# Regrouping the column widths of a streaming skewness kernel: 31 loads instead of 27, same bytes

## Chip, cores and metric

The kernel runs on one core of a Trainium2 chip. The metric is the device time of one execution in microseconds. Unless said otherwise, a quoted time is the median of a kernel's runs. "Faster" or "slower" ask for more than 2%, which is 1.8 us here.

## The reference

```python
rows, cols = 1024, 8192                      # x: float32, standard normal
mean = np.mean(x, axis=-1, keepdims=True)
std = np.std(x, axis=-1, keepdims=True)
z = (x - mean) / (std + 1e-8)
return np.mean(z ** 3, axis=-1)              # skewness of each row
```

## The kernel before

The 1024 rows are eight blocks of 128 rows. Each block of 8192 columns is loaded in tiles of the widths in `UNITS`. For each tile, ACT squares it and sums the squares, DVE multiplies the squares by x and sums the cubes, and PE transposes it into an accumulator for the sum of x. Tiles wider than 2304 columns are squared and cubed in two pieces.

```python
UNITS = [
    [4096, 4096], [4096, 4096], [4096, 4096], [4096, 4096],
    [3584, 2304, 2304],
    [2304, 2304, 2048, 1536],
    [1664, 1792, 1920, 1664, 1152],
    [1024, 1024, 1152, 1280, 1408, 1152, 1152],
]
SUB_MAX = 2304
X_BUFS = 8
# ... cut ...
xt = xpool.tile([P, w], FP, tag="x", name=f"x_{b}_{k}")
nc.sync.dma_start(out=xt, in_=xv[b, :, c0 : c0 + w])            # L140
for s, e in _slices(w):
    # sq is in SBUF; in PSUM ("sqps") for the very last tile
    nc.scalar.activation(out=sq, in_=xt[:, s:e], func=AF.Square,  # L147
        scale=s_scale, accum_out=s2u[:, j : j + 1])
    nc.vector.scalar_tensor_tensor(out=cube, in0=sq, scalar=1.0,  # L152
        in1=xt[:, s:e], op0=ALU.mult, op1=ALU.mult,
        accum_out=s3u[:, j : j + 1])
# ... PE transposes of xt into tp (L165) ...
# after each block: tsb <- tp (ACT, L174), s1ps <- tsb x ones (PE, L175)
# blocks 6 and 7 are closed by small ACT steps (L123 to L128), the last one writes s3u;
# then num <- sum of s3u (DVE, L189), skew (DVE, L192), output DMA (L193)
```

Of the kernel before, what the change touches and what calls it, by code (L numbers as in the profile page):

```python
# [14 lines left out]
UNITS = [  # L15
    [4096, 4096],
    [4096, 4096],
    [4096, 4096],
    [4096, 4096],
    [3584, 2304, 2304],  # L20
    [2304, 2304, 2048, 1536],
    [1664, 1792, 1920, 1664, 1152],
    [1024, 1024, 1152, 1280, 1408, 1152, 1152],
]
S1_ACT = {(0, 0): 1024, (1, 0): 1024, (2, 0): 1024}
SUB_MAX = 2304
# [197 lines left out]
```

## Time and profile before

| | before |
|---|---|
| median time | 91.67 us (91.57 to 91.84, 3 runs); with the later runs of the comparison 91.71 us |
| span in the profile | 89.7 us |
| DMA: rate at 8:40 us, rate at 67:77 us | 429, 413 GB/s |
| last tile landed | 83.56 us |
| DVE's last cube done, ACT's last correction done | 86.60, 86.73 us |
| output DMA issued | 87.23 us |

The prediction below reads the profile's lines of this kernel. Two habits matter. A busy share says little where four engines are all near 80%: what counts is which wait ends last. And a full DMA row tells that nothing is gained by feeding the queue better. The landing times in this document are the trace's own record of the completion of each load.

### The profile page before, as it was taken

How to read it: one execution, taken by the hardware profiler on the slowest of the kernel's cores; microseconds unless marked ns; L12 is line 12 of the kernel's file. 1: busy time of each engine (PE TensorE's matmuls, PEld its weight loads, DVE VectorE, ACT ScalarE, POOL GpSimd, SP SyncE). 2: the span in 40 equal slices, each digit the busy share in tenths (PEclk: the TensorE clock that was granted, in tenths of full speed). 3: DMA queues.
4: the chain of work that ended last, by engine and by line, in shares of the span. 5: the costliest groups of instructions: out<-in, count | busy, mean ns of one | idle time of the engine just before them, and what ended most of it. 6: DMA issues, size and time to landing. Idle time of an engine off the chain costs nothing.

```text
span 89.7 us, 1368 instructions
## 1 busy us (share of the span) xinstructions
PE 64.9 (72%) x504; PEld 59.3 (66%) x504; DVE 72.7 (81%) x80; ACT 72.1 (80%) x106; POOL 11.3 (13%) x14
## 2 busy tenths in 40 slices
PE   0003999892882919989998988888987798969710
PEld 0003999791872909979897977877876787848500
DVE  1000498989999298995999999999999999999970
ACT  6003999699991999859898989978979898999950
POOL 3000000000000000000000000000005999900030
PEclk9999999999999997599999999999999999999998
DMA  3999999999999999999999999999999999994000
GB/s 117 351 424 438 424 431 431 431 431 424 446 416 431 424 438 424 424 438 427 415 409 418 419 427 419 421 415 419 409 414 417 404 413 411 421 412 161 0 0 2
DMA packets 4038, 33.64 MB, mean 375 GB/s; under 512 B 576, under 2 KB 576, under 8 KB 2240
## 3 DMA queue, kind: packets, MB, share of 16 engines
q1 hardware_dynamic: 4032, 33.56, 89.7%
q8 instruction: 4, 0.07, 0.3%
q14 instruction: 2, 0.02, 0.0%
HBM read 33.55 MB, written 0.00 MB: 374 GB/s over the span
## 4 chain that ended last, share of the span: by engine, by line
DMA 73%; ACT 13%; issue 5%; DVE 4%; SPq 1%; PE 1%; DVEq 0%; ACTq 0%
DMA x<-in_x_dram 73%; ACT sq L147 9%; DVE sq L152 3%; ACT sqps L147 1%; ACT same L159 1%; SPq L140 1%; PE s1ps L175 1%; ACT tsb L174 0%; ACT s3u L128 0%; ACT v L127 0%; ACT var L125 0%; DVE num L189 0%; ACT m1sq L124 0%; DVE skew L192 0%; ACT nm L126 0%
## 5 line engine op out<-in xcount | busy, mean ns | idle before, releaser
L152 DVE SCALAR_TENSOR_TENSOR sq<-sq,x 128x2048 f32<-128x2048 f32 (+9 forms) x35 | 70.7, 2071 | 13.4 <-ACT sq L147 13.3
L165 PE MATMUL tp<-ident,x 128*128 128x128 f32 x488 | 62.6, 288 | 17.3 <-DMA x<-in_x_dram 17.2
L165 PEld LDWEIGHTS tp<-ident,x 128*128 128x128 f32 x488 | 57.9, 150 | 20.9 <-DMA x<-in_x_dram 12.7
L147 ACT ACTIVATE sq<-x 128x2048 f32<-128x2048 f32 (+9 forms) x35 | 60.6, 1734 | 10.7 <-DMA x<-in_x_dram 9.9
L110 POOL TENSOR_TENSOR vara<-m2a,m1sqa 128x6 f32<-128x6 f32 x1 | 1.8, 1822 | 67.1 <-DVE m3a L99 67.1
L147 ACT ACTIVATION_READ_ACCUMULATOR sq<-x 128x1 f32 x35 | 6.5, 186 | 0.0
L175 PEld LDWEIGHTS s1ps<-onesn,tsb 128*128 128x128 f32 x16 | 2.4, 188 | 5.2 <-ACT tsb L174 5.2
L175 PE MATMUL s1ps<-onesn,tsb 128*128 128x1 f32 x16 | 3.1, 260 | 3.3 <-ACT tsb L174 3.3
L174 ACT COPY tsb<-tp 128x128 f32<-128x128 f32 x8 | 2.0, 256 | 2.0 <-PE tp L165 2.0
L114 POOL TENSOR_TENSOR rra<-vara,expo 128x6 f32<-128x6 f32 x1 | 3.3, 3267 | 0.0
L159 ACT ACTIVATE same<-x 128x1024 f32<-128x1024 f32 x3 | 3.1, 1041 | 0.0
L152 DVE DVE_READ_ACCUMULATOR sq<-sq,x 128x1 f32 x35 | 2.9, 83 | 0.0
L111 POOL TENSOR_TENSOR m1sq3a<-m1sq3a,vara 128x6 f32<-128x6 f32 x1 | 1.9, 1868 | 0.1
L77 ACT ACT_TABLE_LOAD x1 | 1.3, 1283 | 0.7 <-PEq L208 0.7
L187 POOL TENSOR_TENSOR rr<-var,expo 128x2 f32<-128x2 f32 x1 | 0.7, 702 | 7.7 <-ACT var L125 7.7
L152 DVE SCALAR_TENSOR_TENSOR cube<-sqps,x 128x1152 f32<-128x1152 f32 x1 | 1.4, 1350 | 0.0
L113 POOL TENSOR_TENSOR m3a<-m3a,m1sq3a 128x6 f32<-128x6 f32 x1 | 1.2, 1201 | 0.1
L147 ACT ACTIVATE sqps<-x 128x1152 f32<-128x1152 f32 x1 | 1.1, 1136 | 0.1
L115 POOL TENSOR_TENSOR skew<-m3a,rra 128x6 f32<-128x6 f32 x1 | 1.1, 1069 | 0.1
L124 ACT ACTIVATE m1sq<-s1ps 128x1 f32<-128x1 f32 x2 | 0.3, 171 | 0.5 <-PE s1ps L175 0.5
L75 DVE MEMSET onesn<- 128x1 f32 x1 | 0.1, 59 | 0.8 <-PEq L208 0.8
L112 POOL TENSOR_TENSOR m1sq3a<-m1sq3a,nm1a 128x6 f32<-128x6 f32 x1 | 0.7, 697 | 0.0
(28 smaller groups left out, 6.8 us busy)
## 6 DMA issues: line engine op xcount, KB each, us to landing
x<-in_x_dram SPq DMA_DIRECT2D x8, 2048.0 KB, 23.4
x<-in_x_dram SPq DMA_DIRECT2D x4, 1152.0 KB, 27.9
x<-in_x_dram SPq DMA_DIRECT2D x4, 576.0 KB, 8.6
x<-in_x_dram SPq DMA_DIRECT2D x1, 1792.0 KB, 33.0
x<-in_x_dram SPq DMA_DIRECT2D x2, 832.0 KB, 13.9
x<-in_x_dram SPq DMA_DIRECT2D x1, 1024.0 KB, 21.1
x<-in_x_dram SPq DMA_DIRECT2D x2, 512.0 KB, 10.0
x<-in_x_dram SPq DMA_DIRECT2D x1, 960.0 KB, 13.2
```

The lines of the kernel that those rows point to most:

```text
L77: nc.scalar.activation(out=tiny, in_=onesn, func=AF.Square)
L110: g.tensor_tensor(out=var, in0=m2, in1=m1sq, op=ALU.subtract)
L111: g.tensor_tensor(out=m1sq3, in0=m1sq3, in1=var, op=ALU.add)
L113: g.tensor_tensor(out=m3, in0=m3, in1=m1sq3, op=ALU.add)
L114: g.tensor_tensor(out=rr, in0=var, in1=expo, op=ALU.pow)
L115: g.tensor_tensor(out=skew[:, 0:F], in0=m3, in1=rr, op=ALU.mult)
L147: nc.scalar.activation(out=sq, in_=xt[:, s:e], func=AF.Square, scale=s_scale, accum_out=s2u[:, j : j + 1],)
L152: nc.vector.scalar_tensor_tensor(out=cube, in0=sq, scalar=1.0, in1=xt[:, s:e], op0=ALU.mult, op1=ALU.mult, accum_out=s3u[:, j : j + 1],)
L159: nc.scalar.activation(out=same[:, 0:w_act], in_=xt[:, w - w_act : w], func=AF.Copy, scale=inv_n, accum_out=s1a[:, b : b + 1],)
L165: nc.tensor.matmul(out=tp, lhsT=xt[:, c * P : (c + 1) * P], rhs=ident, start=(k == 0 and c == 0), stop=(c0 == C and c == n - 1), is_transp ...
L174: nc.scalar.copy(out=tsb, in_=tp)
L175: nc.tensor.matmul(out=s1ps[:, b : b + 1], lhsT=tsb, rhs=onesn, start=True, stop=True)
```

## The change

Its apparent intent is to let tiles shrink earlier, so that ACT and DVE wait less for whole 2 MB tiles, and to end on a narrower tile. Nothing but the list of widths changes.

```diff
 UNITS = [
     [4096, 4096],
     [4096, 4096],
-    [4096, 4096],
-    [4096, 4096],
-    [3584, 2304, 2304],
-    [2304, 2304, 2048, 1536],
-    [1664, 1792, 1920, 1664, 1152],
-    [1024, 1024, 1152, 1280, 1408, 1152, 1152],
+    [3456, 1792, 2944],
+    [2944, 2304, 2944],
+    [2944, 2688, 2560],
+    [1920, 1920, 1792, 1536, 1024],
+    [1536, 1408, 1408, 1152, 1408, 1280],
+    [1152, 1152, 1408, 1152, 1280, 1152, 896],
 ]
```

## The prediction

> **What bounds the kernel now.** I began with the page's activity in 40 slices, because four engines are busy 72 to 81% of the span and none of them is the limit by share alone.
>
> ```profile
> DVE  1000498989999298995999999999999999999970
> ACT  6003999699991999859898989978979898999950
> DMA  3999999999999999999999999999999999994000
> GB/s 117 351 424 438 424 431 431 431 431 424 446 416 431 424 438 424 424 438 427 415 409 418 419 427 419 421 415 419 409 414 417 404 413 411 421 412 161 0 0 2
> ```
>
> One digit is a slice of 2.24 us. The DMA row is full from slice 1 to slice 35: there is no hole that another order of transfers could fill. DVE and ACT have holes, and they lie early (slices 10, 12, 18), where they wait for whole 2 MB tiles. The second thing to see is that the rate sinks from about 430 to about 412 GB/s while the transfers become narrower.
>
> The chain that ended last, on the page and then in order of time:
>
> ```profile
> DMA 73%; ACT 13%; issue 5%; DVE 4%; SPq 1%; PE 1%; DVEq 0%; ACTq 0%
> ...
> 76.01 0.02 SPq L140
> 76.03 0.03 issue
> 76.06 7.50 DMA x<-in_x_dram
> 83.56 0.02 issue
> 83.58 1.26 ACT sqps L147 x2
> 84.84 0.00 issue
> 84.84 0.28 ACT tsb L174
> ...
> 86.44 0.30 ACT s3u L128
> 86.74 0.02 issue
> 86.76 0.18 DVE num L189
> ```
>
> So: loading ends at 83.56 us, then follows a serial tail, of which only the first 1.26 us (the squares of the last 1152 columns) depends on the widths. The stretch from 84.84 to the end is fixed small work. The chain goes through a DVE-released buffer at 76.06, but that issue lands 7.5 us later: behind it stood five more transfers of block 7 (1152+1280+1408+1152+1152 = 6144 columns, 3.15 MB, 7.6 us at 412 GB/s). The queue was full, so the buffer wait cost nothing.
>
> Last, the end of DVE in the timeline of the last microseconds:
>
> ```profile
> 83.58 1.14 ACT L147 ACTIVATE sqps<-x 128x1152 f32<-128x1152 f32 x1
> ...
> 85.24 1.35 DVE L152 SCALAR_TENSOR_TENSOR cube<-sqps,x 128x1152 f32<-128x1152 f32 x1
> ...
> 86.52 0.08 DVE L152 DVE_READ_ACCUMULATOR cube<-sqps,x 128x1 f32 x1
> 86.76 0.17 DVE L189 TENSOR_REDUCE num<-s3u 128x2 f32<-128x16 f32 x1 [0.16 <-ACT s3u L128]
> ```
>
> DVE is done at 86.60, ACT's last correction at 86.74: DVE is 0.14 us from being the limit, since it starts the last cube at 85.24, half a microsecond after ACT has the squares (84.75). The list of waits puts 13.3 us of DVE idle on ACT, 9.2 of it before the first tile; the other 4.1 us lie before 41.4 us.
>
> **What the Trainium skill says.** "DMA: Bandwidth & Descriptors", section "Where 436 GB/s comes from", gives 435 GB/s as the ceiling of the SBUF ports; the trace's 429 to 434 GB/s in the wide stretch stands right below it. The same page, section "Why small descriptors are slow (HBM only)", says that each packet carries a fixed overhead; the trace agrees in kind and gives the size used below. "Perfetto Trace Analysis", section "DMA Optimizations", says that splitting may help if the DMA engines are generally idle; here they are not. "ScalarE: Activation LUTs", section "What ACT_TABLE_LOAD costs", gives 186 ns + 0.833 ns per column for an ACTIVATE, back-to-back ones overlapping by 93 ns: 1146 ns for 1152 columns, where the trace has 1136 to 1155.
>
> **The change, part by part.** Bytes, matmuls and the small work stay.
>
> (1) Transfers: 27 become 31. Each has 128 rows, and the packet count (4032 on the queue = 27x128 rows + 128 output rows + 28x16 completions) shows one packet per row, eight per DMA engine. I price a packet from two windows of the DMA view. From 8 to 40 us: 838 row packets of 16 KB (934 less 96 small ones), 16 engines x 32 us x 1.003 = 513.5 engine-us, 613 ns each. From 67 to 77 us: 817 row packets, 4.13 MB, so 5055 B each, 16 x 10 x 1.017 = 162.7 engine-us, 199 ns each. A straight line through both has 0.0365 ns per byte and 15 ns per packet. Check: 58 to 67 us has 532 packets of 7030 B in 144.4 engine-us, 271 ns each; the line says 271. Hence a transfer costs 8 x 15 = 0.12 us plus 1.17 ns per column. Four more transfers: 4 x 0.12 = **+0.47 us** on the landing of the last one. This is fully on the path, because DMA never rests.
>
> (2) Slices: pieces over 2304 columns are halved. Before: 4x4+4+4+5+7 = 36. After: 4+4+5+5+6+5+6+7 = 42, six more. In the timeline an ACT slice costs 0.833 ns per column + 0.20 us from start to start (1.27 for 1280), a DVE slice 1.04 + 0.08 us (1.42 for 1280). So ACT gets 6 x 0.20 = 1.2 us and DVE 6 x 0.08 = 0.5 us. Both lie beside DMA: a block of 8192 columns takes DMA about 9.8 us, ACT 6.8 + 5 x 0.2 + some 0.5 = 8.3 (+1.05 in the first three blocks for the partial sum), DVE 8.5 + 5 x 0.08 = 8.9. They stay below it. **0 on the path.**
>
> (3) The last width: 1152 becomes 896. The squares shrink by 256 x 0.833 = **-0.21 us**, if ACT is free when it lands. With the transfer cost of (1), the last four widths 1152, 1280, 1152, 896 land at L-4.23, L-2.62, L-1.16 and L. ACT takes 1.27 for the 1280 (to L-1.33) and 1.16 for the 1152 from its landing (to L+0.0). ACT is free just in time, so the saving counts. DVE, even if it runs without a gap, ends the 1280 at about L+0.4, the 1152 at L+1.7 and the 896 at L+2.7; ACT's correction comes at 3.18-0.21 = L+2.97. So ACT still closes.
>
> (4) Earlier landings in blocks 2 to 4: a first tile of 3456 instead of 4096 lands 640 x 1.17 = 0.75 us earlier, and the first of block 3 some 1152 x 1.17 = 1.3 us. That fills part of DVE's early idle, and about pays for the 0.5 us of new slice cost. Its backlog does not carry the end, so **0** again.
>
> Sum: +0.47 - 0.21 = +0.26 us on 91.67, or 91.93. I choose a little less, **91.85**, because the falling rate may in part be a drift: 433, 429, 428 GB/s in the windows 8:18, 18:28, 28:38, where the width does not change.
>
> **The rivals.** (a) *The granularity gain is real*: early idle of ACT and DVE (4.1 us of DVE) vanishes and the time falls with it. For it: the holes in their rows, and the page on splitting. Against: their idle is not on the chain; DMA is full while they wait. At best DVE's 0.14 us distance grows. If in addition packets cost nothing extra, the time is 91.67-0.21 = 91.45. (b) *Buffer starvation*: eight buffers hold fewer bytes when the tiles are narrow, and the queue runs dry. For it: 64.2 us of waits for DVE in the queue's own list. Against: block 7 of before already ran so, with five transfers of about 1200 columns ahead, 7 us of work, while DMA stayed full. The changed blocks 4 to 6 are wider than that, 1024 to 2944. A dry spell would cost 1 to 3 us: 93 to 95. (c) *DVE becomes the bound*: it runs without a hole from 43 us to 86, and gets 29 slices instead of 24 in blocks 3 to 7, +0.4 us. If it gained nothing from (4), its end would be 86.60 + 0.4 - 0.27 (shorter last cube) = 86.73, still no later than L+2.97 = 87.0. Only a lag in ACT, as when the granted clock dipped to 0.83 from 28 to 38 us and the copy of the sums waited 1.48 us for PE, could make this worse; I give it +0.3.
>
> **Range and chances.** Between rival (a) with free packets (91.45, less 0.2 for run to run) and my sum with rival (c) (92.2, plus 0.2) lies the range 91.2 to 92.5. Two per cent is 1.83 us. Faster than 89.84 would need the landing at 81.7 at an unchanged tail, with loads that fill the ports already: 1 to 2%. Slower than 93.5 needs (b): 2 to 3%.
>
> **What would show it.** In the changed profile: the DMA row full to the end of loading; 4608 packets on the queue (31x128 + 128 + 32x16) and a last landing near 84.0 (step 1); rates of 416 to 424 where blocks 2 to 4 travel, instead of about 428; 41 + 1 squares and cubes (step 2); an ACT sqps of about 0.92 us that starts within 0.1 us of the landing (step 3); fewer DVE holes in slices 12 to 18 (step 4); the closing reduction still released by ACT. The prediction is wrong if the DMA row shows a gap, if the last landing comes earlier than 83.4, or if the reduction is released by DVE's cube.

## The result, and the profile after

The changed kernel took 91.89 us (median of 4 runs, 91.88 to 92.15), the kernel before 91.71 us in the same comparison. The ratio is 1.0027, with a 95% interval of 1.0004 to 1.0050. A ratio is the mean time of one kernel's runs over that of the other's of the same rounds, so it is not quite the ratio of the medians. The change costs about 0.25 us. The predicted 91.85 us was right to 0.04 us, and the outcome lies within 2%.

From the page of the changed kernel, activity of DVE and DMA in 40 slices of 2.25 us:

```profile
DVE  1000598989899597999998999999999999779980
DMA  4899999999999999999999999999999999994000
```

DMA is full to the end of loading, as before. DVE's early holes are shallower, but it has new ones in slices 34 and 35 (77 to 81 us), just where nothing can be made up any more. Its total wait for ACT is 13.3 us in both kernels: idle time was moved, not removed.

The chain that ended last, from the page and in order of time:

```profile
DMA 52%; issue 13%; DVE 12%; ACT 10%; PE 9%; SPq 1%; DVEq 0%; ACTq 0%
...
84.91 1.36 DVE sq L152 x3
86.28 1.02 DVE cube L152 x2
```

The chain no longer ends on a landing followed by ACT: it ends on DVE's cubes. The timeline of the last block (start, duration, instruction, and in brackets the idle time of the engine before it and who ended it) shows how that came about:

```profile
77.32 1.36 DVE L152 SCALAR_TENSOR_TENSOR sq<-sq,x 128x1152 f32<-128x1152 f32 x1 [0.38 <-ACT sq L147]
77.83 0.29 ACT L128 ACTIVATE s3u<-v,nm 128x1 f32<-128x1 f32 x1
78.03 1.15 ACT L147 ACTIVATE sq<-x 128x1152 f32<-128x1152 f32 x1
79.31 1.36 DVE L152 SCALAR_TENSOR_TENSOR sq<-sq,x 128x1152 f32<-128x1152 f32 x1 [0.62 <-ACT sq L147]
84.10 0.90 ACT L147 ACTIVATE sqps<-x 128x896 f32<-128x896 f32 x1
86.19 1.09 DVE L152 SCALAR_TENSOR_TENSOR cube<-sqps,x 128x896 f32<-128x896 f32 x1
86.60 0.29 ACT L128 ACTIVATE s3u<-v,nm 128x1 f32<-128x1 f32 x1
87.39 0.17 DVE L189 TENSOR_REDUCE num<-s3u 128x2 f32<-128x16 f32 x1
```

DVE waits 0.38 and 0.62 us for the squares of the first two tiles of block 7; from 79.31 on it works without a gap to 87.28. ACT's last correction is done at 86.89. Before, the last two stood at 86.60 and 86.73, with ACT closing. For comparison, the second tile of block 7 in before:

```profile
77.22 1.04 ACT L147 ACTIVATE sq<-x 128x1024 f32<-128x1024 f32 x1
78.26 0.28 ACT L128 ACTIVATE s3u<-v,nm 128x1 f32<-128x1 f32 x1
78.39 1.22 DVE L152 SCALAR_TENSOR_TENSOR sq<-sq,x 128x1024 f32<-128x1024 f32 x1
```

The squares of this tile start 0.81 us later in the changed kernel (78.03 against 77.22) and the cube 0.92 us later (79.31 against 78.39). The order of ACT's instructions differs too: before, the last small step of block 6 (L128) comes after these squares, in the changed kernel ahead of them. Of the 0.81 us, 0.38 were there when the first tile's squares started, 0.12 are their greater width, and 0.31 lie between the two tiles, where that step now stands.

One more difference lies behind the computation. In the list of waits of the sync engine, the wait for the output's DMA at the end of the program is 1.1 us in before and 0.8 us after, though the output takes 1.4 us from issue to landing in both. First before, then after:

```profile
SPq L219 <- DMA out_dram<-skew: 1.1, 1, 1.1
```

```profile
SPq L219 <- DMA out_dram<-skew: 0.8, 1, 0.8
```

So three things moved, and between the two profiled runs they add up:

| | before | after | difference |
|---|---|---|---|
| last tile landed | 83.56 | 83.85 | +0.29 |
| from there to the closing reduction | 3.20 | 3.54 | +0.34 |
| from the output's landing to the end | 1.08 | 0.83 | -0.25 |
| time of these two runs | 91.50 | 91.88 | +0.38 |

The profiled run of before, 91.50 us, was faster than the four runs of the comparison (91.57 to 91.84), hence +0.38 here and +0.25 over all runs. A landing scatters from one execution to the next: the five other kernels with 27 large loads in the trials below landed their last tile between 83.57 and 83.94. Over all six the mean is 83.69, over the five traces with 31 loads it is 83.91 (83.75 to 84.08), so row 1 is nearer to +0.2 than +0.3. The experiments therefore test each row by its own means.

**Theory.** A load costs something (row 1), the narrow last tile saves nothing since DVE closes, because of the new grouping of block 7, which starts wider (row 2), and the number of DMAs changes the end of the program (row 3). **Rival**, the prediction's own account: four loads at 0.12 us, less 0.21 us for the narrow tile, and nothing else.

### The profile page after: what moved, and what is told of

Read it like the earlier page. It is cut to its first block, busy times and chain, and to the rows that moved or that the text cites. A ratio compares the mean times of both kernels' runs of the same rounds, so it can differ in the third digit from the quotient of the medians.

```text
span 90.1 us, 1408 instructions
## 1 busy us (share of the span) xinstructions
PE 65.2 (72%) x504; PEld 59.3 (66%) x504; DVE 73.6 (82%) x92; ACT 73.3 (81%) x118; POOL 9.1 (10%) x14
## 4 chain that ended last, share of the span: by engine, by line
DMA 52%; issue 13%; DVE 12%; ACT 10%; PE 9%; SPq 1%; DVEq 0%; ACTq 0%
DMA x<-in_x_dram 52%; DVE sq L152 10%; PE tp L165 8%; ACT sq L147 7%; SPq L140 1%; ACT same L159 1%; DVE cube L152 1%; ACT tsb L174 0%; PE s1ps L175 0%; ACT v L127 0%; ACT var L125 0%; DVE num L189 0%; ACT nm L126 0%; DVE skew L192 0%; ACT m1sq L124 0%
## 5 line engine op out<-in xcount | busy, mean ns | idle before, releaser
L152 DVE SCALAR_TENSOR_TENSOR sq<-sq,x 128x1408 f32<-128x1408 f32 (+9 forms) x41 | 71.6, 1798 | 13.3 <-ACT sq L147 13.3
L147 ACT ACTIVATE sq<-x 128x1408 f32<-128x1408 f32 (+9 forms) x41 | 61.9, 1512 | 9.8 <-DMA x<-in_x_dram 9.2
L147 ACT ACTIVATION_READ_ACCUMULATOR sq<-x 128x1 f32 x41 | 7.6, 187 | 0.0
L110 POOL TENSOR_TENSOR vara<-m2a,m1sqa 128x6 f32<-128x6 f32 x1 | 0.2, 198 | 66.4 <-DVE m3a L99 66.4
L152 DVE DVE_READ_ACCUMULATOR sq<-sq,x 128x1 f32 x41 | 3.4, 83 | 0.0
L114 POOL TENSOR_TENSOR rra<-vara,expo 128x6 f32<-128x6 f32 x1 | 2.7, 2720 | 0.0
L152 DVE SCALAR_TENSOR_TENSOR cube<-sqps,x 128x896 f32<-128x896 f32 x1 | 1.1, 1089 | 0.0
L147 ACT ACTIVATE sqps<-x 128x896 f32<-128x896 f32 x1 | 0.9, 897 | 0.0
L127 ACT ACTIVATE v<-m1sq,var 128x1 f32<-128x1 f32 x2 | 0.6, 295 | 0.1
```

Source lines behind the costliest of these rows:

```text
L114: g.tensor_tensor(out=rr, in0=var, in1=expo, op=ALU.pow)
```

## The experiments

A difference is the mean of a kernel's runs less the mean of all runs of before in that session on the same chip; in parentheses stand the ratio, which takes the same rounds alone, and its interval. The two can disagree by up to 0.1 us. Comparisons between two trials go through before, since they were not timed against each other. All results are correct, except for the two marked.

### Block 7 alone

```diff
-    [1024, 1024, 1152, 1280, 1408, 1152, 1152],
+    [1152, 1152, 1408, 1152, 1280, 1152, 896],     # blocks 0 to 6 as before
```

> Blocks 0 to 6 as before, block 7 as in the changed kernel; still 27 transfers. Theory (two terms: 0.12 us per transfer on the landing, and a tail that DVE now closes because ACT releases the second cube of block 7 late): the last landing stays at 83.5 +/- 0.15 us, the closing reduction is released by DVE's cube and not by ACT, and the time is +0.1 to +0.3 us on before although the last tile is narrower. Rival of the prediction's sum (ACT closes, the narrow last tile saves 0.21 us): time -0.2 us, reduction released by ACT.

Measured: 91.87 us, +0.24 us (1.0019, 1.0003 to 1.0034). By the ratio it is +0.17 us, with an interval from +0.03 to +0.31. Block 7 alone, with its narrow end, costs about what the whole change costs, against the rival's -0.2. The profiled run was the kernel's slowest, 92.13 us, and its tile landed late, at 83.94 us, outside what I had expected (its first tile was already 0.2 us late). The order at the end does not depend on that. From its timeline:

```profile
79.32 1.36 DVE L152 SCALAR_TENSOR_TENSOR sq<-sq,x 128x1152 f32<-128x1152 f32 x1 [0.29 <-ACT sq L147]
...
86.20 1.09 DVE L152 SCALAR_TENSOR_TENSOR cube<-sqps,x 128x896 f32<-128x896 f32 x1
86.66 0.29 ACT L128 ACTIVATE s3u<-v,nm 128x1 f32<-128x1 f32 x1
87.40 0.17 DVE L189 TENSOR_REDUCE num<-s3u 128x2 f32<-128x16 f32 x1
```

DVE gets the squares of its second cube of block 7 at 79.32 as in the changed kernel, runs through, and the reduction starts at 87.40 (changed kernel: 79.31, 87.39).

### Blocks 2 to 6 alone

The changed kernel with block 7 as before: 31 loads, 42 pieces.

> Blocks 2 to 6 as in the changed kernel, block 7 as before; 31 transfers. Theory: four more transfers at 0.12 us put the last landing 0.3 to 0.5 us later, ACT closes as before 3.2 us after the landing, time +0.3 to +0.5 us. Rival (packets cost nothing, the fall of the rate is a drift in time): landing and time within 0.1 us of before, or less where earlier landings help.

Measured: 91.64 us, -0.02 us (0.9997, 0.9981 to 1.0012). My expectation was missed. The four loads and six pieces seem to cost nothing, which looks like a win for the rival "packets cost nothing". But in the profiled run the last tile landed 0.52 us later than in before, at 84.08, the reduction followed 3.20 us after it as in before, and the output was issued 0.52 us later. The run was only 0.27 us slower (91.77 against 91.50), because the end of the program was 0.25 us shorter, as in the changed kernel. With that 0.25 us taken off, the times leave 0.23 us for the four loads. This miss is what led to row 3.

### A price for loads: eight more

```diff
-    [4096, 4096],            # blocks 0 to 3
+    [2048, 2048, 2048, 2048],
```

The pieces of ACT and DVE stay the same 36.

> Before, with blocks 0 to 3 loaded as 2048-column tiles: 35 transfers instead of 27, and the very same 36 squares and cubes. Theory: 8 x 0.117 = +0.94 us on the last landing and about as much on the time (+0.7 to +1.0); the rate in the first half drops from 429 to about 421 GB/s. Rival (drift in time, not packets): the first half stays at 429 GB/s, landing and time as before or earlier.

Measured: 92.07 us, +0.45 us (1.0047, 1.0029 to 1.0066), half of what I expected. The last landing was at 84.09, +0.53 us. From 8 to 40 us the DMA moved 422 GB/s instead of 429, so the falling rate is not a drift in time: it follows the width. Loads do cost, but 0.066 us each by this landing, not 0.117.

### A price for loads: 24 more

```diff
-            nc.sync.dma_start(out=xt, in_=xv[b, :, c0 : c0 + w])
+            q = 1024 if w == 4096 else w
+            for p0 in range(0, w, q):
+                nc.sync.dma_start(out=xt[:, p0 : p0 + q], in_=xv[b, :, c0 + p0 : c0 + p0 + q])
```

Here tiles and buffers stay as well.

> The price of a transfer by itself: before with each of its eight 4096-column tiles filled by four loads of 1024 columns instead of one; tiles, buffers, squares and cubes are the same, 51 large transfers and 52 DMAs in all (again 4 over a multiple of eight, so the end is as in before). The prediction's price (0.117 us per transfer) says +2.8 us on the landing and the time. The price read from the landings of the run with eight more (0.06 us) says +1.4 us. No price: 0.

Measured: 94.42 us, +2.67 us (1.0301, 1.0267 to 1.0336), with runs from 93.53 to 94.65. By time this seems to agree with the prediction's price. By the landing, 85.51 in place of 83.56, it is 1.95 / 24 = 0.081 us. In the middle of the load, four 1024-column loads land in 5.11 us where one of 4096 columns takes 4.88: 0.077 us per extra load. The profiled run (93.97 us) was 2.47 us slower than before's, of which 0.4 us lie in the end of the program, in another of the sync engine's waits; if every run had these, the time leaves 2.27 / 24 = 0.09 us per load. This run differs in one more way: its sync engine waited 26.8 us for earlier loads before issuing further ones, before's not at all, though its DMA row shows no gap. I can't say what the remaining scatter of a microsecond is. The landings of both trials put the price at 0.07 to 0.08 us per load.

### The narrow last tile with a narrow start

```diff
-    [1024, 1024, 1152, 1280, 1408, 1152, 1152],
+    [1024, 1024, 1280, 1280, 1408, 1280, 896],     # blocks 0 to 6 as before
```

> Before, with block 7 as 1024, 1024, 1280, 1280, 1408, 1280, 896: the same narrow last tile as the changed kernel, but the first two tiles of block 7 as narrow as before. Theory (DVE runs without a gap from its second cube of block 7, and that one is set by ACT): DVE ends where it ended before (86.6 +/- 0.15 us), ACT's correction 0.2 us earlier, so the time is -0.15 to 0 us on before. Rival (the narrow last tile saves its 0.21 us wherever it stands): -0.2 us here and in the run with block 7 alone.

Measured: 91.59 us, 0.00 us (0.9998, 0.9982 to 1.0014). The last tile landed at 83.57, ACT's correction was done at 86.68, and DVE's cube at 86.70. The ACT side gained only 0.05 us, since ACT starts the last squares 0.3 us after the landing, being busy with a 1280-column tile. Both sides now end together, and the narrow tile saves nothing in this grouping either. Other groupings were not tried.

### Block 7 regrouped inside the changed kernel

```diff
-    [1152, 1152, 1408, 1152, 1280, 1152, 896],
+    [1024, 1024, 1280, 1280, 1408, 1280, 896],     # blocks 0 to 6 as in the changed kernel
```

> The changed kernel with block 7 as 1024, 1024, 1280, 1280, 1408, 1280, 896: only block 7 regrouped, the last tile stays 896, still 31 transfers. Theory (the wide first two tiles of block 7 make ACT release the second cube late and DVE never catches up): -0.2 us against the changed kernel, i.e. 0 +/- 0.1 us on before. Rival (the four extra transfers make the changed kernel slower, block 7 has no part): +0.25 us on before, as the changed kernel.

Measured: 91.58 us, -0.07 us on before (0.9989, 0.9974 to 1.0005), so some 0.3 us below the changed kernel with the same 31 loads and the same last width. In its timeline DVE starts the second cube of block 7 at 78.35, close to before's 78.39 and 0.96 us ahead of the changed kernel:

```profile
78.35 1.23 DVE L152 SCALAR_TENSOR_TENSOR sq<-sq,x 128x1024 f32<-128x1024 f32 x1 [0.38 <-ACT sq L147]
...
86.89 0.17 DVE L189 TENSOR_REDUCE num<-s3u 128x2 f32<-128x16 f32 x1
```

The reduction follows the landing (83.75) by 3.14 us instead of 3.54. The grouping of block 7 is the cause of row 2. Here, as in before, the step of L128 stands after the second tile's squares. The trials change the whole grouping and with it ACT's order, so how much is due to the width of the first tiles and how much to the order is not shown.

### Who closes: half of the last cube

```diff
+                h = (e - s) // 2 if last_unit else e - s
                 nc.vector.scalar_tensor_tensor(
-                    out=cube, in0=sq, scalar=1.0, in1=xt[:, s:e],
+                    out=cube[:, 0:h], in0=sq[:, 0:h], scalar=1.0, in1=xt[:, s : s + h],
```

This leaves out half of the last tile's cubes, so its result is wrong. On the changed kernel:

> The changed kernel, but the very last cube is taken over half of its 896 columns (wrong result on purpose). Theory: in the changed kernel DVE closes, 0.4 us behind ACT's last correction, so taking 0.47 us of DVE work off the end moves the time by about -0.4 us against the changed kernel, i.e. -0.15 +/- 0.1 us on before, and ACT is then the releaser of the closing reduction. Rival (ACT closes as predicted): no change against the changed kernel, +0.25 us on before.

Measured: 91.45 us, -0.19 us on before (0.9980, 0.9964 to 0.9995), that is 0.43 us below the changed kernel. A removal of 0.47 us of DVE work (1.09 to 0.62 us) is paid out almost in full: DVE closed. The control on before, wrong result too:

> Control: before with the same halving of its last cube (1152 to 576 columns, wrong result on purpose). ACT closes here with 0.14 us to spare, so the time stays within 0.1 us of before. If the reduction was limited by DVE in before too, the time falls by some 0.5 us.

Measured: 91.54 us, -0.11 us (0.9985, 0.9971 to 1.0000; four runs). Here 0.6 us of DVE work were removed, and about a fifth shows (the interval allows 0 to 0.27 us); I had expected at most 0.1. In its trace DVE then waits for ACT:

```profile
86.81 0.17 DVE L190 TENSOR_REDUCE num<-s3u 128x2 f32<-128x16 f32 x1 [0.78 <-ACT s3u L128]
```

The tenth of a microsecond at the edge of the interval may mean that DVE closes in some runs of before; the two ends are only 0.13 us apart. That stays open.

### The end of the program: four tiny loads

Each DMA in the trace names the semaphore that it raises. There are eight in these two kernels, used in turn (101, 103, 105 to 110). At its end the sync engine waits for them in five instructions, in the same order in both kernels. The trace's record (start in us, semaphores waited for), before on the left, changed kernel on the right:

```text
output raises 106 (28th DMA)          output raises 110 (32nd DMA)
88.67  106, 105   <- output landed    88.25  106, 105
88.73  107, 103                       88.31  107, 103
88.79  108, 101                       88.37  108, 101
88.86  109, 100                       88.44  109, 100
88.92  110, 104                       89.29  110, 104   <- output landed
```

With 28 DMAs the output is on the first wait, and four more follow it, 63 ns each. With 32, a multiple of eight, it is on the last one, and the others are over before it lands. The landing records of all traces bear this out: from the output's landing to the end of the span it is 0.83 us in the six kernels with 32 DMAs, 1.08 or 1.09 us in the six with 28 or 36, and 1.49 us in the one with 52. To test it without changing the large loads, four loads of 16 numbers each, which nothing reads, were put into before:

```diff
             c0 += w
+            if b == 3 and k == 1:
+                for t in range(4):
+                    bit = small(f"bit{t}", 1)
+                    nc.sync.dma_start(out=bit[0:16, :], in_=xv[0, 0:16, t : t + 1])
```

> Before with four extra loads of 16 single numbers each, which nothing reads: 32 DMAs in all instead of 28, the same bytes and the same 27 large transfers otherwise. Theory (at the end the sync engine waits for eight DMA semaphores in a fixed order; with a total that is a multiple of eight the output is on the last of them, the four other waits of 63 ns each are behind it before it lands, 0.25 us are saved): -0.15 to -0.25 us on before. In this trace the wait for the output at the end shows 0.8 us instead of 1.1. Rival (the 0.3 us shorter end of the changed kernel is chance, or comes from something else in it): 0 or a little more, as there are four more DMAs.

Measured: 91.47 us, -0.16 us (0.9978, 0.9964 to 0.9992): four more DMAs make the kernel slightly faster. The tiny loads are not quite neutral: the sync engine now waits 36 us in all for earlier loads before it issues others (in before for none), and the last tile of the profiled run landed at 83.84, +0.28 us, at the edge of the scatter. The end of the program is 0.25 us shorter all the same. From its list of waits of the sync engine (the line number is shifted by the edit):

```profile
SPq L223 <- DMA out_dram<-skew: 0.8, 1, 0.8
```

The counter-test puts the same four into the changed kernel, 36 DMAs:

> The changed kernel with four extra loads of 16 numbers each that nothing reads: 36 DMAs, no multiple of eight any more. Theory: the changed kernel has been helped by 0.25 us at its end, and loses that again: +0.2 to +0.3 us against the changed kernel, +0.4 to +0.6 us on before, and 1.1 us of waiting for the output at the end in place of 0.8. Rival: within 0.1 us of the changed kernel, +0.25 us on before.

Measured: 92.54 us, +0.89 us (1.0100, 1.0085 to 1.0115), so some 0.6 us above the changed kernel, more than the 0.25 us expected. The wait is 1.1 us again, as the theory says. The span grew by 0.3 to 0.4 us; the rest lies outside it: time less span is 1.75 to 2.13 us in these runs, and 1.75 to 1.81 in those of the changed kernel. That part has no explanation in the profile, so this run confirms the direction and not the size.

### A candidate that beats both

The regrouped block 7 with the last width 896, and the four tiny loads, on before.

> Candidate for a kernel faster than both: before with block 7 as 1024, 1024, 1280, 1280, 1408, 1280, 896 and the four tiny loads (32 DMAs, 27 large transfers). Theory: the end saves 0.25 us, the narrow last tile nothing, as DVE closes: -0.2 to -0.3 us on before, about as the four tiny loads alone.

Measured: 91.52 us, -0.12 us (0.9989, 0.9977 to 1.0002). I had expected -0.2 to -0.3. It is no better than the tiny loads alone, which remain the one version with a right result whose interval lies below before's time, by 0.2%. That is a curiosity of the end of the program, not a better kernel.

## Why the prediction was right or wrong

The number was right and the outcome was right by luck: errors in opposite directions cancelled. By a sign that the prediction had named itself, "the reduction is released by DVE's cube", its mechanism was wrong. What held and what failed, step by step (L is the landing of the last tile):

- **What bounds the kernel** held: DMA is full to the end of loading, no buffer wait starves it, rivals (a) and (b) did not come.
- **Step 1**, "Four more transfers: 4 x 0.12 = +0.47 us", was right in mechanism and too large. The trials priced a load at 0.07 to 0.08 us by the landings, so about 0.3 us for four; the changed kernel's landing came 0.29 us later, and 0.21 us lie between the mean landings. A similar price comes from the average of the 16 DMA engines: in the windows from 80 us on, the DMA share (next to last column) says how long the average engine still works.

```profile
80.00:81.00 1.00, 0.58 (x6) 0.35 (x5) 1.00 (x1) 1.00 (x3) 0.00 (x0) 1.00 1.07 423
81.00:82.00 1.00, 1.00 (x11) 1.00 (x10) 1.00 (x3) 1.00 (x1) 0.00 (x0) 1.00 0.48 194
82.00:83.00 1.00, 1.00 (x10) 0.77 (x9) 1.00 (x3) 1.00 (x3) 0.00 (x0) 1.00 0.15 60
```

These are before's; the shares sum to 1.70 us. The changed kernel's:

```profile
80.00:81.00 1.00, 1.00 (x9) 0.80 (x8) 1.00 (x3) 1.00 (x3) 0.00 (x0) 1.00 1.03 414
81.00:82.00 1.00, 0.62 (x6) 0.58 (x6) 1.00 (x1) 1.00 (x3) 0.00 (x0) 1.00 0.79 304
82.00:83.00 1.00, 0.88 (x8) 0.64 (x7) 1.00 (x3) 1.00 (x3) 0.00 (x0) 1.00 0.24 95
83.00:84.00 1.00, 1.00 (x10) 0.92 (x10) 1.00 (x3) 1.00 (x2) 0.00 (x0) 1.00 0.05 18
```

  They sum to 2.11 us, 0.41 more, which looks near the predicted 0.47. But before's is the lowest of the six traces with 27 large loads (1.70 to 1.99, mean 1.83). The five with 31 have 2.07 to 2.18 (mean 2.13), the one with eight more 2.43, the one with 24 more 3.71: 0.07 to 0.08 us per load in each case. The working itself has a likely reason for the excess: it multiplied its two windows by their shares, 1.003 and 1.017. A share above 1 means that packet times on an engine overlap, so the overlap was counted twice. Without these factors the same two windows give 611 and 196 ns, hence 10.6 ns per packet and 0.085 us per load. This is an estimate made afterwards.
- **Step 2** (six more pieces, nothing on the path) held on the whole; no run isolates it.
- **Step 3**, "ACT is free just in time, so the saving counts", failed, in sign too. ACT started the last squares 0.25 us after the landing, and DVE, put at L+0.4 for the 1280 columns and L+2.7 for the end, was done at L+1.14 and L+3.43. I had followed ACT and DVE only through the last four tiles, and given DVE too little backlog. Its backlog comes from the start of the block, where ACT has 1152 columns instead of 1024 twice, with block 6's small steps between. ACT did not close; DVE did, 0.4 us after it. The tail cost +0.34 us in place of -0.21.
- **Step 4** (earlier landings fill DVE's idle) was half right: DVE's wait for ACT before 41 us and the one at 41.4 us shrank from 13.3 to 11.6 us, and 1.7 us came back later, 1.0 us of them in block 7 (13.3 us in both kernels). My text also misread the rows of before: slice 10 has no hole; DVE's early ones are at 13 and 18, ACT's at 7, 12 and 17.
- **Missing altogether**: the end of the program, -0.25 us, set by the number of DMAs modulo eight, of which only the remainders 0 and 4 were run. I had listed the stretch from 84.84 to the end as fixed.
- **Rival (c)**, DVE becomes the bound, was given up to +0.3 us and put down to a lag in ACT. This is what happened, with another cause of the lag than the granted clock.

In sum I had +0.47 - 0.21 = +0.26, less 0.08 for a drift that the run with eight more loads did not show; the two traces show +0.29 + 0.34 - 0.25 = +0.38, with the mean landings +0.30, and the runs +0.25.

## What to carry to other kernels

Where two engines end as close together as here (0.13 us), do not count on a shorter last tile by itself: follow each engine through the whole last block, from its first tile, and ask which one will then close. A predicted time that comes true proves none of its terms; only runs that change one term at a time do. And a comparison of two variants with different numbers of DMAs can carry a difference at the program's end that has nothing to do with the work, here 0.25 us between 28 or 36 DMAs and 32.

## What the Trainium skill lacked or had wrong

- "DMA: Bandwidth & Descriptors", section "Why small descriptors are slow (HBM only)", gives a fixed overhead per packet and calls packing worthwhile only at 256 B or less; it gives no time for loads with rows of several KB. Here a load of 128 rows of 4 to 16 KB cost 0.07 to 0.08 us more than the same bytes within a larger one, and the rate was 429 GB/s with 16 KB rows and 422 with 8 KB rows.
- The same page, section "Rules for kernel authors", says to dedicate one semaphore to a DMA, but not that the end of a program waits for all of them in order. Eight in turn, with the output on the last rather than the first, saved 0.25 us here.
